# One operand of each later first product made seven steps early into held tiles, and the P2 sum of the second product kept in PSUM over all quarters

## The chip, the core and the metric

The kernel runs on one NeuronCore of a Trainium2 chip. TensorE (PE) multiplies, its weight loads (PEld) overlap the multiplications; ScalarE (ACT) and VectorE (DVE) do the elementwise work, GpSimd (POOL) and SyncE (SP) mostly issue transfers. The metric is the device time of one execution in microseconds (us), the median of the runs. Each engine takes its instructions in the order of its own queue and waits at an instruction whose input is not ready.

## The reference

A model of two layers on 512 tokens of width 1024, in float32. Layer 0 mixes with stick-breaking attention, layer 1 with a gated linear recurrence; after each mixer comes the MLP that this change touches.

```python
def squared_relu_mlp(h, w1, w2):
    u = jax.nn.relu(h @ w1)
    return (u * u) @ w2

def reference(x, norm_mix, norm_mlp, mlp_w1, mlp_w2, ...):
    ...
        x = x + y
        h = rms_norm(x, norm_mlp[layer])
        x = x + squared_relu_mlp(h, mlp_w1[layer], mlp_w2[layer])
    return rms_norm(x, norm_final)
```

`w1` is 1024 x 4096, `w2` is 4096 x 1024, for each layer.

## The kernel before

A float32 product is made of three matmuls of rounded halves. An operand is copied to a rounded high half by ACT (`wh`, `bh`, `sh`: a CAST row), the rest is subtracted by DVE (`wl`, `bl`, `sl`: a TENSOR_TENSOR row), and PE adds high x high, low x high and high x low. `operand` (L1091) does this for a weight block, `split` and `split_slot` for an activation.

The hidden width of 4096 is worked off in four quarters of 1024. In each, the products are done by a scheme with seven block products in place of eight (P1 to P7), which add and subtract blocks: `added` (L1109) adds one block of weights onto another, by DVE (`b<-b,b`) or, for P7 and P4 and one P6, by a POOL transfer that adds. `PRODUCTS` says for each which block of the activations and which blocks of the weights it takes (`b11`, `b12`, `b21`, `b22`), and to which sum it goes: X (P1, P6, P7, P4), V (P5, P3) or W (P2). Only P2 takes `b21`, which no other product needs: `source` (L1100) loads it into a tile of its own, `raw`, of which there are three.

A quarter has 28 steps, counted by `place` (L1186); a layer starts at place 14 of quarter 0, whose first product is done in another way.

- Places 0 to 6 are the first product (up) for the first half of the quarter's hidden width, in the order P1 P5 P6 P3 P7 P2 P4; places 7 to 13 are the same for the second half. A step is 24 matmuls of 256 columns. Each result is read from PSUM by ACT (a COPY row) or by an add on DVE (`u<-ps,u`, `u<-u,ps`), then relu and square on ACT make the activations of the second product, which are split into halves again (`bh`, `bl` for the first half, `sh`, `sl` for the second).
- Places 14 to 27 are the second product (down), with sums over both halves: P1 0, P5 0, P1 1, P2 0, P5 1, P6 0, P6 1, P3 0, P3 1, P7 0, P7 1, P2 1, P4 0, P4 1, where 0 and 1 name the half. A step is 12 matmuls of 512 columns. `collect` (L1140) scales a finished sum and adds it onto the output `c` on DVE (the first time on ACT).

PE's order is written out by `run` (L1172), and the orders of ACT and DVE follow it there too, since each of their instructions in an MLP is issued behind the one before (`Ordered`). For step i, `load(i)` issues transfers, `leave(i - 1)` reads the step before and calls `prepare(i + 3)`, and then PE's matmuls of step i are issued. Leaving step i thus prepares step i + 4: `prepare` (L1220) makes that step's operand (and the one before it, if that was left out: P7's waits for a POOL transfer) and does the additions that the next steps need. A weight operand lives in a ring of four pairs of `wh` and `wl`.

PSUM has eight banks under four names with two each: o, t, a (acc) and z. `bank` (L857) deals them in a fixed turn, `BANKS`. Each quarter takes two for its W sum, and its `collect` at place 25 frees them.

Of the kernel before, what the change touches and what calls it, by code (L numbers as in the profile page):

```python
# [13 lines left out]
F32R = mybir.dt.float32r  # L14
# [4 lines left out]
P = 128  # L19
S = 512  # L20
D = 1024
C = D // P
# [45 lines left out]
def hybrid_encoder(  # L68
# [27 lines left out]
    wpool = ctx.enter_context(tc.tile_pool(name="wpool", bufs=4))  # L96
# [138 lines left out]
    wpools, rawpools = [wpool], [wpool]  # L235
    slabs, loads = count(), count()
# [91 lines left out]
    with ExitStack() as actx:  # L328
# [26 lines left out]
        q, kh, kl, v, w = {}, {}, {}, {}, {}  # L355
# [73 lines left out]
        sums = work.tile([P, S], F32, tag="ssq", name="ssq", bufs=1)  # L429
# [303 lines left out]
        steps = chain(*(g for g, _ in fill))  # L733
# [51 lines left out]
    NQ = DFF // D  # L785
# [22 lines left out]
    class Mlp:  # L808
# [28 lines left out]
        def __init__(self, ctx, layer):  # L837
            self.layer, self.sq, self.first = layer, Squares(), None
            self.V, self.A = Ordered(V), Ordered(A)
            self.mp = ctx.enter_context(tc.tile_pool(name=f"mlp{layer}", bufs=2))  # L840
            self.c = [
                self.mp.tile([P, 2, S], F32, tag=f"c{i}", name=f"c{i}", bufs=1) for i in range(4)
            ]
            self.begun, self.a, self.aside = set(), {}, {}
            self.turns = count(4 * layer)
            self.blocks = ExitStack()
            self.bp = self.blocks.enter_context(tc.tile_pool(name=f"blocks{layer}", bufs=2))
            self.u, self.lows, self.s3, self.slots = {}, {}, {}, None
# [6 lines left out]
            return self.c[t // 2 * 2 + h][:, t % 2, :]  # L855

        def bank(self):  # L857
            tag = self.BANKS[next(self.turns) % 8]
            return bank("acc" if tag == "a" else tag)


# [226 lines left out]
                self.FROM_UP,  # L1088
            )

        def operand(self, raw):  # L1091
            pool = wpools[next(slabs) % len(wpools)]
            wh = pool.tile([P, C, P], F32R, tag="wh", name="wh")
            wl = pool.tile([P, C, P], F32R, tag="wl", name="wl")
            wh, wl = (t.rearrange("p (j k) f -> p j (k f)", j=2) for t in (wh, wl))
            self.A.copy(wh, raw)
            self.V.tensor_tensor(wl, raw, f(wh), ALU.subtract)
            return wh, wl
# [62 lines left out]
        def part(self, sums, name, g, w):  # L1161

            to = self.PRODUCTS[name][3]
            if to not in sums:
                sums[to] = [self.bank() for _ in range(2)]
            for i in range(2):
                self.times(name, g, i, w, sums[to][i], name in ("P1", "P5", "P2"))

        UP = "P1", "P5", "P6", "P3", "P7", "P2", "P4"
        STEPS = 28  # L1170

        def run(self, first, between, end):  # L1172
# [5 lines left out]
            steps = []  # L1178
# [5 lines left out]
            units, ws, sums, us = {("down", 0): first}, {}, {}, {}  # L1184
# [25 lines left out]
            def make(i):  # L1210
                if i >= len(steps):
                    return
                name = steps[i][3]
                ws[i] = made[i] = self.operand(self.source(unit(i), name))

                for before, x in (("P5", "P7"), ("P6", "P4")):
                    if name == before:
                        self.added(unit(i), x)

            def prepare(i):  # L1220

                if i < len(steps) and steps[i][0] == "up" and steps[i][3] == "P7":
                    return
                if i - 1 in range(len(steps)) and i - 1 not in made and i > 2:
                    make(i - 1)
                if i < len(steps) and steps[i][0] == "down":
# [11 lines left out]
            def load(i):  # L1238
                q4, at = steps[i][1], place(i)
                for do in self.aside.get(i, ()):  # L1240
                    do()

                if i == 0:
                    self.turns = count(2)
                elif at == 0:
                    self.turns = count(4)
                    self.u.clear()
                    del self.a[1]
                elif at == 4:
# [12 lines left out]
            def leave(i):  # L1262

                ahead = i + 4
                if i < 0:
                    return
                kind, q4, p, name = steps[i]
                bank = sums[kind, q4, p if kind == "up" else 0][self.PRODUCTS[name][3]]
                if kind == "down":
                    if q4 == 0 and self.s3 and place(i) in self.REPLACE:  # L1270
                        self.replace()
                    apart = p and name == "P2" and self.layer and q4 == NQ - 1
                    if p and not apart:
                        self.collect(name, 0, bank[0])
                    if steps[min(ahead, len(steps) - 1)][0] == "down":
                        add(ahead, 0)
                    if p and not apart:
# [12 lines left out]
                    return  # L1290
# [6 lines left out]
                if keep is not None:  # L1297

                    self.A.copy(cut(u[keep]), three)
                at, x, y, op = {  # L1300
                    "P3": (1, three, cut(u[1]), ALU.subtract),
                    "P7": (2, cut(u[2]), cut(u[3]), ALU.subtract),
                    "P2": (0, cut(u[0]), three, ALU.add),
                    "P4": (3, three, None, None),
                }.get(name, (None,) * 4)
# [36 lines left out]
                elif name in ("P5", "P6") and p:  # L1342
                    n = ("P5", "P6").index(name)
# [20 lines left out]
            for i, (kind, q4, g, name) in enumerate(steps):  # L1364
# [10 lines left out]
                to = self.PRODUCTS[name][3]  # L1375
                new = to not in banks
# [33 lines left out]
    with ExitStack() as mctx:  # L1410
# [7 lines left out]
        def feature(c, tag):  # L1418

            pt = bank(tag)  # L1420
            for t in range(NB):
                PE.transpose(
                    pt[:, t * P : (t + 1) * P], mlp.y(t, c // 4)[:, c % 4 * P : (c % 4 + 1) * P],
                    ident,
                )
            V.tensor_tensor(x[c], x[c], pt, ALU.add)
            last["low"] = halves("mix1", c, x[c])

        def end(ws, xs):
            x_down(0, 0)  # L1430
            for i in range(2):
                for g in range(2):
                    mlp.times("P4", g, i, ws[g], xs[i], False)
                mlp.collect("P4", i, xs[i])
                if i == 0:
                    for c in range(4, C):
                        feature(c, "zzoo"[c - 4])
                        squares.chunk(c, x[c], e=G)

        def between(c):  # L1440
# [35 lines left out]
    with ExitStack() as rctx:  # L1476
# [36 lines left out]
        ps, xc, aa, a0, om, z, gin, pg = ({} for _ in range(8))  # L1513
# [4 lines left out]
        ws = {"c2": third}  # L1518
        raws, fetched, made = {}, count(), count(3)
# [375 lines left out]
```

## Time and profile before

| what | value |
|---|---|
| median of 3 runs (lowest to highest) | 1001.99 us (1001.78 to 1002.32) |
| the profiled execution | 1003.18 us |
| its span, from the first to the last instruction | 1001.3 us |
| an MLP's quarter, place 17 to place 17 | 74.75 us |
| casts of weight blocks `wh<-b` on ACT | 168, 1048 ns each |
| their `wl<-b,wh` on DVE | 168, 1220 ns each |
| loads of `raw` from `w_dn` on SP's queue | 16, 512 KB each, 4.9 us to landing |

A row of the timeline gives the start in us, the duration in us, the engine, the line, the operation, what is written and read, the shape, and in brackets how long the engine was idle before and what it waited for. Much of the MLP has L798, the helper that records every operation, so that its rows are told apart by their tiles. ps_t, ps_acc, ps_o and ps_z are the banks by name. The durations of matmuls overlap; the distance of two starts is what a matmul costs. A row of a window gives the stretch, its length, and for PE, PEld, DVE, ACT and POOL the busy time and the count, then the granted clock and the share of the DMA engines.

### The profile page before, as it was taken

What the parts mean: (1) busy time and instruction counts of PE and PEld (TensorE: products, weight loads), DVE (VectorE), ACT (ScalarE), POOL (GpSimd) and SP (SyncE); (2) the same over time, 40 slices, a digit from 0 to 9 for tenths busy, and PEclk for the clock granted to TensorE, in tenths of its full rate; (3) what the DMA queues carried; (4) which work ended last, traced back from release to release, by engine and by line L of the source; (5) the groups of instructions that cost most, each with busy time, mean ns of one, the idle gap of its engine ahead of it and who ended that gap; (6) DMA issues with size and microseconds to landing.
All of it is one profiled execution on the core that took longest, in us unless ns stands there. A gap on an engine that the chain in (4) does not pass through costs nothing.

```text
span 1001.3 us, 15918 instructions
## 1 busy us (share of the span) xinstructions
PE 983.0 (98%) x5836; PEld 884.0 (88%) x5836; DVE 858.0 (86%) x1152; ACT 715.4 (71%) x1110; POOL 176.4 (18%) x243
## 2 busy tenths in 40 slices
PE   9999999999999999999999999999999999999996
PEld 7889999888878988988988888888889989989985
DVE  6888787848898799799799799986887898998898
ACT  6777676836887774774775699975887774874865
POOL 0454444420000011011011220100011111111111
PEclk9999999999999999999999999999999999999999
DMA  7855454537637767777693474446548877977953
GB/s 230 216 146 148 106 153 109 160 117 256 174 87 198 169 160 198 169 163 194 169 239 88 128 191 126 124 157 223 122 95 219 212 142 202 249 141 199 229 107 106
DMA packets 71902, 165.72 MB, mean 166 GB/s; under 512 B 23824, under 2 KB 25104, under 8 KB 71824
## 3 DMA queue, kind: packets, MB, share of 16 engines
q1 hardware_dynamic: 59424, 123.54, 39.4%
q0 software_dynamic: 11680, 40.38, 24.0%
q8 instruction: 46, 0.75, 0.3%
q10 hardware_dynamic: 720, 0.79, 0.2%
q14 instruction: 32, 0.26, 0.1%
HBM read 139.51 MB, written 6.29 MB: 146 GB/s over the span
## 4 chain that ended last, share of the span: by engine, by line
PE 39%; DVE 25%; ACT 22%; issue 8%; DMA 6%; SPq 0%; ACTq 0%; POOL 0%; DVEq 0%; POOLq 0%
PE ps_t L1135 8%; DVE wl L798 6%; ACT wh L798 6%; PE ps_acc L1135 4%; DVE u L798 4%; ACT u L798 3%; PE ps_acc L1036 3%; DVE b L798 3%; PE ps_acc L257 3%; PE ps_acc L259 3%; PE ps_acc L258 2%; PE ps_z L1135 2%; ACT bh L798 2%; DVE c L798 2%; ACT L798 2%
## 5 line engine op out<-in xcount | busy, mean ns | idle before, releaser
L798 ACT CAST wh<-b 128x1024 fp32r<-128x1024 f32 x168 | 173.7, 1048 | 99.6 <-DVE b L798 50.1
L798 DVE TENSOR_TENSOR wl<-b,wh 128x1024 fp32r<-128x1024 f32 x168 | 203.6, 1220 | 38.9 <-ACT wh L798 38.5
L1113 POOL DMA_DIRECT2D b<-in_w_dn x40 | 35.0, 876 | 339.6 <-DVE b L798 153.1
L1036 PE MATMUL ps_z<-xg,wh 128*128 128x256 f32 x384 | 78.2, 277 | 1.0 <-ACT u L798 1.0
L257 PE MATMUL ps_acc<-xg,wh 128*128 128x512 f32 x200 | 79.1, 395 | 0.0
L259 PE MATMUL ps_acc<-xg,wh 128*128 128x512 f32 x200 | 75.8, 379 | 0.0
L258 PE MATMUL ps_acc<-xg,wl 128*128 128x512 f32 x200 | 75.8, 379 | 0.0
L251 DVE TENSOR_TENSOR wl<-raw,wh 128x512 fp32r<-128x512 f32 (+2 forms) x70 | 62.0, 911 | 15.1 <-ACT wh L249 14.8
L798 ACT ACTIVATE u<-u 128x512 f32<-128x512 f32 x100 | 63.2, 632 | 13.3 <-DVE u L798 11.6
L623 DVE TENSOR_TENSOR_SCAN scan<-keep,later 128x128 f32<-128x128 f32 (+1 forms) x64 | 59.3, 929 | 12.9 <-ACT keep L613 6.5
L1036 PE MATMUL ps_z<-xg,wl 128*128 128x256 f32 x240 | 66.0, 275 | 0.0
L1036 PEld LDWEIGHTS ps_z<-xg,wh 128*128 128x128 f32 x384 | 63.5, 192 | 1.7 <-ACT u L798 1.6
L249 ACT CAST wh<-raw 128x512 fp32r<-128x512 f32 (+2 forms) x70 | 50.5, 757 | 19.1 <-PE ps_acc L259 6.8
L627 POOL TENSOR_TENSOR w<-w,scan 128x128 f32<-128x128 f32 (+1 forms) x64 | 51.6, 807 | 53.6 <-DVE scan L623 50.6
L1036 PE MATMUL ps_acc<-xg,wh 128*128 128x256 f32 x288 | 60.5, 275 | 0.0
L798 DVE TENSOR_TENSOR b<-b,b 128x1024 f32<-128x1024 f32 x48 | 58.7, 1223 | 1.3
L798 DVE TENSOR_TENSOR u<-u 128x512 f32<-128x512 f32 (+1 forms) x92 | 54.8, 595 | 2.3 <-ACT u L798 1.0
L1113 POOL DMA_DIRECT2D b<-in_w_up x24 | 20.9, 869 | 196.8 <-DMA b<-in_w_up 84.4
L1036 PE MATMUL ps_acc<-xg,wl 128*128 128x256 f32 x192 | 52.8, 275 | 0.0
L1036 PE MATMUL ps_acc<-low,wh 128*128 128x256 f32 x192 | 52.8, 275 | 0.0
L798 ACT CAST wh<-raw 128x1024 fp32r<-128x1024 f32 x46 | 47.9, 1043 | 4.1 <-PE ps_acc L1135 4.0
L1135 PE MATMUL ps_t<-wh,sl 128*128 128x512 f32 x126 | 48.5, 385 | 1.9 <-DVE sl L798 1.9
(372 smaller groups left out, 3257.9 us busy)
## 6 DMA issues: line engine op xcount, KB each, us to landing
b<-in_w_dn SPq DMA_DIRECT2D x48, 512.0 KB, 5.1
b<-in_w_dn POOLq DMA_DIRECT2D x40, 512.0 KB, 5.5
b<-in_w_up SPq DMA_DIRECT2D x36, 512.0 KB, 4.7
b<-in_w_up POOLq DMA_DIRECT2D x24, 512.0 KB, 5.8
raw<-in_w_m SPq DMA_DIRECT2D x16, 512.0 KB, 4.7
raw<-in_w_dn SPq DMA_DIRECT2D x16, 512.0 KB, 4.9
raw<-in_w_in SPq DMA_DIRECT2D x16, 512.0 KB, 4.2
raw<-in_w_qk SPq DMA_DIRECT2D x12, 512.0 KB, 3.7
```

The lines of the kernel that those rows point to most:

```text
L249: A.copy(wh[:, k, :], raw[:, k, :])
L251: V.tensor_tensor(wl[:, k, :], raw[:, k, :], f(wh[:, k, :]), ALU.subtract)
L257: PE.matmul(ps, wh, ah, start=start, stop=False)
L258: PE.matmul(ps, wl, ah, start=False, stop=False)
L259: PE.matmul(ps, wh, al, start=False, stop=stop)
L623: V.tensor_tensor_scan(sc[:, S - n : S][:, ::-1], keep[:, :n][:, ::-1], later[:, S - n :][:, ::-1], 1.0, ALU.mult, ALU.max,)
L627: G.tensor_tensor(wt, wt, sc[:, S - n + 1 : S + 1], ALU.mult)
L798: ins = getattr(self.e, name)(*args, **kwargs)
L1036: PE.matmul(as_read(ps[:, i * HS : (i + 1) * HS]), m, turns_of(y), start=new and i == k == n == 0, stop=i == 1 and k == C // 2 - 1 and n == 2,
L1113: G.dma_start(out=unit[b].rearrange("p j n -> p (j n)"), in_=unit["src"](to), accum_op=ALU.add)
L1135: PE.matmul(ps, m, y[:, jj], start=first and n == 0, stop=last and n == 2, skip_group_check=not new,)
```

## The change

Two things are done, in both layers.

**One operand early.** The operand of place 12 (P2 of the second half, quarters 1 to 3) is made when place 5 is left, not place 8. Its halves go to two tiles, `spare`, that are taken once from the three `raw` buffers and held over the quarters. Leaving places 8 to 11 then prepares the step five ahead (so 13, 14, 15 and 16), leaving place 12 prepares nothing, and leaving place 13 goes on as before with 17.

**One sum kept.** The W sum of the second product (P2) stays in its two banks from quarter 0 to 3. The matmuls go on adding, and the `collect` of P2 is left out in quarters 0 to 2. Two banks are so held over the whole MLP (both of z), and the other six are dealt from written lists, `planned`, by quarter. Layer 0's last two transposes before the next mixer (`feature`) take a bank of acc and one of t in place of two of o.

```diff
-            self.turns = count(4 * layer)
+            self.spare = None
+            self.kept, self.growing = None, False
+            self.planned = []
+            self.turns = count(2 + 2 * layer)
...
         def bank(self):
-            tag = self.BANKS[next(self.turns) % 8]
+            tag = self.planned.pop(0) if self.planned else self.BANKS[next(self.turns) % 8]
...
-        def operand(self, raw):
-            pool = wpools[next(slabs) % len(wpools)]
-            wh = pool.tile([P, C, P], F32R, tag="wh", name="wh")
-            wl = pool.tile([P, C, P], F32R, tag="wl", name="wl")
+        def operand(self, raw, spare=False):
+            if spare:
+                self.spare = self.spare or [
+                    wpool.tile([P, C, P], F32R, tag="raw", name="spare", bufs=3) for _ in range(2)
+                ]
+                wh, wl = self.spare
+            else:
+                pool = wpools[next(slabs) % len(wpools)]
+                wh = pool.tile([P, C, P], F32R, tag="wh", name="wh")
+                wl = pool.tile([P, C, P], F32R, tag="wl", name="wl")
...
             if to not in sums:
-                sums[to] = [self.bank() for _ in range(2)]
+                if to == "W":
+                    self.kept = self.kept or [self.bank() for _ in range(2)]
+                sums[to] = self.kept if to == "W" else [self.bank() for _ in range(2)]
+            new = name in ("P1", "P5") or name == "P2" and not self.growing
+            self.growing = self.growing or name == "P2" and g == 1
...
+        SOONER, MADE = 12, 5
...
+                if i in made:
+                    return
...
-                if i - 1 in range(len(steps)) and i - 1 not in made and i > 2:
-                    make(i - 1)
+                for n in range(max(i - 2, 2), min(i, len(steps))):
+                    make(n)
...
                 if i == 0:
-                    self.turns = count(2)
+                    self.planned[:] = "ooatzz"
                 elif at == 0:
-                    self.turns = count(4)
+                    self.planned[:] = ("", "atatooaatoat", "totoaattoa", "oaoattooatat")[q4]
...
-                ahead = i + 4
                 if i < 0:
                     return
+                at = place(i)
+                ahead = i + 4 + (at in range(self.SOONER - 4, self.SOONER))
+                if at == self.MADE:
+                    make(i + self.SOONER - at)
+                if at == self.SOONER:
+                    ahead = len(steps) + 9
...
+                    grows = name == "P2" and q4 < NQ - 1
...
-                    if p and not apart:
+                    if p and not apart and not grows:
                         self.collect(name, 0, bank[0])
```

What this makes of the queues is shown at three places of quarter 2 of layer 0; the other quarters 1 to 3 read alike.

DVE as place 5 is left. `u<-u,ps` is P2's add of the first half, `bl<-u,bh` the first of its halves for the second product, `wl<-b` the splits of P5 and P6 of the second half. Before:

```order
L798 TENSOR_TENSOR wl<-b_4514,wh 128x1024
L798 TENSOR_TENSOR b_4514<-b_4514,b_4570 128x1024
L798 TENSOR_TENSOR u<-u,ps_z 128x2x256
L798 TENSOR_TENSOR wl<-b_4514,wh 128x1024
L798 TENSOR_TENSOR bl<-u,bh 128x2x768
```

and after:

```order
L798 TENSOR_TENSOR wl<-b_4510,wh 128x1024
L798 TENSOR_TENSOR b_4510<-b_4510,b_4566 128x1024
L798 TENSOR_TENSOR spare<-raw,spare 128x1024
L798 TENSOR_TENSOR u<-u,ps_t 128x2x256
L798 TENSOR_TENSOR wl<-b_4510,wh 128x1024
L798 TENSOR_TENSOR bl<-u,bh 128x2x768
```

The split of place 12 now stands ahead of the add.

DVE as places 9 to 12 are left. `u<-ps,u` is P3's add of the second half, the first `u<-u` P7's, `u<-u,ps` P2's; the last row is the `sl` that P1 1 at place 16 takes. Before, from the second `bl` of the first half:

```order
L798 TENSOR_TENSOR bl<-u,bh 128x1024
L798 TENSOR_TENSOR u<-ps_o,u 128x512
L798 TENSOR_TENSOR wl<-b_4750,wh 128x1024
L798 TENSOR_TENSOR b_4750<-b_4750,b_4752 128x1024
L798 TENSOR_TENSOR u<-u 128x512
L798 TENSOR_TENSOR sl<-u,sh 128x2x256
L798 TENSOR_TENSOR wl<-b_4750,wh 128x1024
L798 TENSOR_TENSOR sl<-u,sh 128x2x256
L798 TENSOR_TENSOR u<-u,ps_o 128x512
L798 TENSOR_TENSOR wl<-b_4754,wh 128x1024
L798 TENSOR_TENSOR b_4754<-b_4754,b_4990 128x1024
L798 TENSOR_TENSOR sl<-u,sh 128x2x256
```

and after:

```order
L798 TENSOR_TENSOR wl<-b_4744,wh 128x1024
L798 TENSOR_TENSOR b_4744<-b_4744,b_4746 128x1024
L798 TENSOR_TENSOR bl<-u,bh 128x1024
L798 TENSOR_TENSOR u<-ps_acc,u 128x512
L798 TENSOR_TENSOR wl<-b_4744,wh 128x1024
L798 TENSOR_TENSOR u<-u 128x512
L798 TENSOR_TENSOR sl<-u,sh 128x2x256
L798 TENSOR_TENSOR wl<-b_4748,wh 128x1024
L798 TENSOR_TENSOR b_4748<-b_4748,b_4987 128x1024
L798 TENSOR_TENSOR sl<-u,sh 128x2x256
L798 TENSOR_TENSOR u<-u,ps_acc 128x512
L798 TENSOR_TENSOR sl<-u,sh 128x2x256
```

The split of place 14 and the addition for place 15 (the first two rows) have moved ahead of P3's add, the split of place 16 and the addition for place 18 ahead of P2's, and nothing stands between P2's add and its `sl`.

SP's queue from the loads of place 4 on, where each `raw` load waits for a free buffer. Before:

```order
L1066 DMA b_4754<-in_w_dn 128x1024
L1066 DMA b_4752<-in_w_dn 128x1024
L1105 DMA raw<-in_w_dn 128x1024
L1066 DMA b_4750<-in_w_dn 128x1024
L1066 DMA b_4990<-in_w_dn 128x1024
L1066 DMA b_4992<-in_w_dn 128x1024
L1105 DMA raw<-in_w_up 128x1024
```

and after:

```order
L1069 DMA b_4748<-in_w_dn 128x1024
L1069 DMA b_4746<-in_w_dn 128x1024
L1114 DMA raw<-in_w_up 128x1024
L1069 DMA b_4744<-in_w_dn 128x1024
L1114 DMA raw<-in_w_dn 128x1024
L1069 DMA b_4987<-in_w_dn 128x1024
L1069 DMA b_4989<-in_w_dn 128x1024
```

The load for place 12 has moved into the same quarter, behind two loads of place 4.

More of the change, by code (lines that the diff above doesn't have):

```diff
@@ L1164, in part @@
             if to not in sums:
-                sums[to] = [self.bank() for _ in range(2)]
+                if to == "W":
[3 more added lines that the diff above has]
+            self.growing = self.growing or name == "P2" and g == 1
             for i in range(2):
-                self.times(name, g, i, w, sums[to][i], name in ("P1", "P5", "P2"))
+                self.times(name, g, i, w, sums[to][i], new)
         UP = "P1", "P5", "P6", "P3", "P7", "P2", "P4"
+        SOONER, MADE = 12, 5
         STEPS = 28
@@ L1212, in make @@
                     return
+                if i in made:
+                    return
                 name = steps[i][3]
-                ws[i] = made[i] = self.operand(self.source(unit(i), name))
+                ws[i] = made[i] = self.operand(self.source(unit(i), name), place(i) == self.SOONER)
                 for before, x in (("P5", "P7"), ("P6", "P4")):
@@ L1276, in leave @@
                         add(ahead, 0)
-                    if p and not apart:
+                    if p and not apart and not grows:
                         self.collect(name, 1, bank[1])
@@ L1436, in end @@
                     for c in range(4, C):
-                        feature(c, "zzoo"[c - 4])
+                        feature(c, ("z", "z", "acc", "t")[c - 4])
                         squares.chunk(c, x[c], e=G)
```

## The prediction

> **What bounds the kernel now.** I read the page first, then the windows of one whole quarter of an MLP, then the timeline of TensorE at the end of that quarter's up products, and last the two engines it waits for there.
>
> ```profile
> span 1001.3 us, 15918 instructions
> PE 983.0 (98%) x5836; PEld 884.0 (88%) x5836; DVE 858.0 (86%) x1152; ACT 715.4 (71%) x1110; POOL 176.4 (18%) x243
> 367.93:442.68 74.75, 74.34 (x505) 68.97 (x505) 67.26 (x74) 49.14 (x63) 7.83 (x9) 1.00 0.72 176
> PE ps_t L1135 <- DVE sl L798: 1.9, 6, 0.3
> ```
>
> TensorE is the bound: the third row is one quarter of layer 0, and PE is busy for 74.34 of its 74.75 us at clock 1.00, DVE (67.26) comes next. The change removes no matmul, so it can only alter how long PE waits. The last row, from the list of who waited for whom, says where that happens six times: the down products (ps_t, L1135) wait for an `sl`, once per quarter 1 to 3 of each layer. The timeline of one such place:
>
> ```profile
> 439.01 0.40 PE L1135 MATMUL ps_t<-wh,sh 128*128 128x512 f32 x1
> 439.25 0.38 PE L1135 MATMUL ps_t<-wl,sh 128*128 128x512 f32 x1
> 439.95 0.48 PE L1135 MATMUL ps_t<-wh,sl 128*128 128x512 f32 x1 [0.32 <-DVE sl L798]
> 440.27 0.38 PE L1135 MATMUL ps_t<-wh,sh 128*128 128x512 f32 x1
> ...
> 442.21 0.38 PE L1135 MATMUL ps_z<-wh,bh 128*128 128x512 f32 x1
> 442.68 0.48 PE L1135 MATMUL ps_z<-wl,bh 128*128 128x512 f32 x1
> 443.00 0.38 PE L1135 MATMUL ps_z<-wh,bl 128*128 128x512 f32 x1
> ```
>
> The first row is where place 16 begins (P1, second half), the 442.21 row where place 17 begins (P2). Matmuls overlap, so a wait is read from starts: undisturbed, one starts 0.216 us after another (the 12 of place 16 take 442.21 - 439.01 = 3.20 us; without the waits that follow, 2.6 = 12 x 0.216). From 439.25 to 439.95 are 0.70, so 0.48 of wait for `sl`, and 0.10 more at the next start (0.32); from 442.21 to 442.68 are 0.47, so 0.25 of wait for `wl`, and again 0.10. **0.94 us a quarter**, 5.6 us in six: this is all that the change can win at this place. It comes from DVE and ACT, which hand work to each other there:
>
> ```profile
> 413.19 1.23 DVE L798 TENSOR_TENSOR b<-b,b 128x1024 f32<-128x1024 f32 x1
> 414.34 0.68 DVE L798 TENSOR_TENSOR u<-u,ps_z 128x512 f32<-128x512 f32 x1
> ...
> 418.30 1.76 DVE L798 TENSOR_TENSOR bl<-u,bh 128x1536 fp32r<-128x1536 f32 x1 [1.47 <-ACT bh L798]
> ...
> 425.02 1.22 DVE L798 TENSOR_TENSOR wl<-raw,wh 128x1024 fp32r<-128x1024 f32 x1
> 426.16 1.22 DVE L798 TENSOR_TENSOR bl<-u,bh 128x1024 fp32r<-128x1024 f32 x1
> ...
> 429.56 0.69 DVE L798 TENSOR_TENSOR u<-ps_o,u 128x512 f32<-128x512 f32 x1
> 430.17 1.22 DVE L798 TENSOR_TENSOR wl<-b,wh 128x1024 fp32r<-128x1024 f32 x1
> 431.42 1.23 DVE L798 TENSOR_TENSOR b<-b,b 128x1024 f32<-128x1024 f32 x1
> 432.56 0.68 DVE L798 TENSOR_TENSOR u<-u 128x512 f32<-128x512 f32 x1
> ...
> 435.60 0.69 DVE L798 TENSOR_TENSOR sl<-u,sh 128x512 fp32r<-128x512 f32 x1 [0.61 <-ACT sh L798]
> 436.21 0.68 DVE L798 TENSOR_TENSOR u<-u,ps_o 128x512 f32<-128x512 f32 x1
> ...
> 439.21 0.69 DVE L798 TENSOR_TENSOR sl<-u,sh 128x512 fp32r<-128x512 f32 x1
> 440.06 1.42 DVE L798 TENSOR_TENSOR u<-u 128x512 f32<-128x512 f32 x2 [0.17 <-ACT u L798]
> 441.40 1.22 DVE L798 TENSOR_TENSOR wl<-raw,wh 128x1024 fp32r<-128x1024 f32 x1
> ```
>
> ```profile
> 414.51 1.06 ACT L798 CAST wh<-b 128x1024 fp32r<-128x1024 f32 x1 [1.42 <-DVE b L798]
> 415.47 1.28 ACT L798 ACTIVATE u<-u 128x512 f32<-128x512 f32 x2
> ...
> 430.29 1.30 ACT L798 ACTIVATE u<-u 128x512 f32<-128x512 f32 x2 [1.03 <-DVE u L798]
> 431.61 0.62 ACT L798 CAST sh<-u 128x512 fp32r<-128x512 f32 x1
> ...
> 436.93 1.30 ACT L798 ACTIVATE u<-u 128x512 f32<-128x512 f32 x2 [0.40 <-DVE u L798]
> 438.26 0.62 ACT L798 CAST sh<-u 128x512 fp32r<-128x512 f32 x1
> 438.78 0.59 ACT L798 ACTIVATE u<-ps_z 128x512 f32<-128x512 f32 x1
> 439.40 0.63 ACT L798 ACTIVATE u<-u 128x512 f32<-128x512 f32 x1
> ```
>
> From 418.30 to 435 DVE has no pause to speak of, yet it takes up the second half's P2 sum (`u<-u,ps_o`) only at 436.21, five us after PE finished it (place 12 ended at 439.01 - 2 x 2.6 - 2.69 = 431.1, an up place being 24 matmuls of 0.112). Behind that add hangs a chain: relu and square, the cast `sh`, then `sl`. PE wants `sh` at 439.01. **The time at which P2's add starts decides the wait.**
>
> **The change, part by part.** I follow DVE through the new order of its queue (the rows under "The change") with the durations above.
>
> *The early split.* Leaving place 5, the operand of place 12 is now cast by ACT and split by DVE ahead of P2's add of the first half. ACT has room: 1.42 us idle before 414.51, the cast takes 1.05. On DVE it stands in front of the add of 414.34 and holds the queue for 1.14 (from 425.02 to 426.16), so the add starts at 415.48 and ends at 416.16. ACT's relu, which ran at 415.47, starts at 416.19: 0.72 later, and with it the cast `bh` and the `bl` of 418.30, now 419.02. The idle 1.47 before that `bl` does not cover it, since that idle time is the wait for this same chain.
>
> *From there to P3's add.* It was 429.56 - 418.30 = 11.26 us of queue. Gone is the place-12 split (1.14). New is the split of place 14 and the addition for place 15, because leaving places 8 to 11 prepares five ahead, not four: 432.56 - 430.17 = 2.39. P3's add starts at 419.02 + 11.26 - 1.14 + 2.39 = 431.53, 1.97 later than before.
>
> *From P3's add to P2's.* It was 436.21 - 429.56 = 6.65, of which 0.61 idle, so 6.04 of work. The new order has the same kinds (two splits, one addition, two `sl`, two adds): 6.04 again. Idle comes in twice. The first `sl` needs `sh`, which is 1.94 behind the end of P3's add (430.29 to 431.61 + 0.62) with 0.04 for each hand-over: 431.53 + 0.69 + 0.04 + 1.94 + 0.04 = 434.24, DVE would be free at 433.87, so 0.37. The next split needs ACT's cast behind that `sh`: another 0.35. P2's add starts at 431.53 + 6.04 + 0.72 = **438.29, where it was 436.21**.
>
> *The wait.* From that add's start to the end of `sh` were 438.26 + 0.62 - 436.21 = 2.67, a chain that no reordering shortens: `sh` is there at 440.96. PE, at place 16 since 439.01, waits 1.95 for it. `sl` ends 0.73 after it, PE wants it 0.43 after: 0.30 more, and 0.10 as above. ACT's relu and square of P4 start 0.52 behind the start of `sh` and end at 442.11; the two sums take 1.34 (440.06 to 441.40), the split of place 17 ends at 443.49 + 1.22 = 444.71. PE begins place 17 at 440.96 + 0.40 + 2.59 = 443.95 and wants that `wl` 0.22 later: 0.58 with its hand-over, and 0.10. Together 3.03 where 0.94 were: **2.09 us a quarter**. The next quarter starts from PE again (DVE has pauses before it, below), so nothing adds up from one to the next: 6 x 2.09 = 12.5 us.
>
> *The kept sum.* Twelve collects go (two in each of quarters 0 to 2 of both layers), a pair taking 394.20 - 392.88 = 1.32 us of DVE.
>
> ```profile
> 392.88 1.40 DVE L798 SCALAR_TENSOR_TENSOR c<-ps_z,rr,c 128x512 f32<-128x512 f32 x2
> 394.20 1.22 DVE L798 TENSOR_TENSOR wl<-b,wh 128x1024 fp32r<-128x1024 f32 x1
> ...
> 397.86 1.23 DVE L798 TENSOR_TENSOR wl<-b,wh 128x1024 fp32r<-128x1024 f32 x1 [1.19 <-ACT wh L798]
> ...
> 403.44 1.23 DVE L798 TENSOR_TENSOR wl<-b,wh 128x1024 fp32r<-128x1024 f32 x1 [1.90 <-ACT wh L798]
> ```
>
> Between them and the up products DVE already pauses for 1.19 and 1.90 us, and PE does not wait: the time falls into a pause. At most it is worth 6 x 1.32 = 7.9 us, if DVE bound there; I take nothing, by the two pauses. Against it stand two banks fewer in turn. The tightest reuse is place 15's second bank, read last by P3's add (ends 432.2 in the new order) and written by PE from 439.01 - 1.3 = 437.7: 5.5 us to spare, nothing again, where a late release would cost PE what it is late.
>
> *One load buffer.* The held tiles take two of the three `raw` slots, so from quarter 2 on the place-12 operand is loaded only when that of place 5 is split.
>
> ```profile
> 401.57 3.45 SPq L1066 DMA_DIRECT2D b<-in_w_dn  x2
> 405.83 0.33 SPq L1105 DMA_DIRECT2D raw<-in_w_dn  x1
> DMA to landing us min/median/max: 4.3/4.4/5.2
> ```
>
> A load is issued at that very point before too, at 405.83, and those of this stretch land within 5.2: 411.0, and ACT wants it at 413.1. It costs nothing with 2 us to spare; behind the waiting cast would stand the relu of 415.47, and each us of lateness beyond would reach PE whole.
>
> *A rule against it.* The windows row grants clock 1.00, and after each wait above the matmuls go on at 0.22 (439.01 to 439.25). The Trainium skill, "TensorE: Matmul & The Clock Gate" (Part 1: The HAM clock gate), says that TensorE falls to half its clock once it was idle for a window of about 3.4 us. By that rule the forecast waits of about 2 us leave the clock alone; by none of the rows here can it be tried, as no wait is as long.
>
> **The rivals.** (1) *The waits go* and nothing replaces them: 6 x 0.94 less, 996.4 us. For it: place 12 has no split left to prepare, and `sl` now stands right behind P2's add. It decides by one point: P2's add must start by 439.01 - 2.67 = 436.34. My chain misses that by two us, and DVE would have to find them between 418 and 436, where it has none. (2) *Nothing measurable*: P2's add lands within some 0.3 us of its old place, because the removed split and the pulled ones cancel: 1002.0. Against it: 2.39 came in, 1.14 went. (3) *Half of it*: the early split slips into a pause and the 0.72 is not passed on; then 1.37 a quarter, 8.2, 1010.2. Against it: the order rows put it ahead of the add, and ACT's cast cannot start before 413.1. (4) *The change does not get its operand early*: the one buffer makes the load late by 1 us or so in the four later quarters, 1018.5. For it: the two loads of 401.57 to 405.0 are still under way when it starts. (5) *The clock*: if a wait of more than three us halves TensorE's rate over the next place of 2.59 us, 6 x 2.59 come on top, 1030.
>
> **How the numbers follow.** The profiled execution took 1003.18 us with its span of 1001.30; 12.5 more are 1015.7. The median of the runs shown is 1001.99, 1.19 below the profiled one, so 1014.5. Chances: forecast (1011 to 1018) 0.68, (3) 0.11, (1) 0.09, (4) 0.06, (2) 0.04, (5) 0.02. Slower by over 0.2% (about what a measurement of this kernel can tell from no change) is forecast, (3), (4) and (5): 0.87; within it 0.04; faster 0.09. The range 1008 to 1019 holds the forecast, most of (3) and part of (4).
>
> **What would show it.** In the profile after: PE's first matmul of place 16 waits for ACT `sh` (not `sl`) about 1.9 us, six times; P2's add of the second half starts within half a us of its `sl` chain with DVE idle some 2 us between them; `c<-ps_z` appears only in the last quarters; place 5 shows a split ahead of `u<-u,ps`. It would be wrong if DVE reached P3's add before 430 in the frame above, if the wait for `sh` is absent, or if PE waits for a bank or a load instead.

## The result, and the profile after

The change makes the kernel slower. Its median is 1018.88 us (1017.25 to 1021.22, four runs); before it was 1002.15 (1001.78 to 1002.64, four runs beside them). The ratio is 1.0168, 95% interval 1.0148 to 1.0189. The profiled execution is the fastest of the four, 1017.25 us.

The head of its page, and the window of one quarter of layer 0 from its place 0 to the next (the columns as before):

```profile
span 1014.7 us, 15901 instructions
PE 985.8 (97%) x5836; PEld 885.3 (87%) x5836; DVE 851.9 (84%) x1140; ACT 715.2 (70%) x1110; POOL 176.4 (17%) x243
395.50:472.20 76.70, 75.22 (x505) 69.18 (x504) 66.08 (x72) 49.25 (x62) 7.85 (x9) 1.00 0.69 172
```

DVE has twelve instructions fewer and is 6 us less busy, PE has the same 5836 matmuls at the same clock, and each quarter is about 2 us longer. The time went into waits of PE. The list of who waited for whom has rows that before had only small ones like them:

```profile
PE ps_o L1039 <- ACT u L798: 4.5, 4, 2.2
PE ps_acc L1039 <- ACT u L798: 2.9, 4, 1.3
PE ps_z L1144 <- DVE wl L798: 2.7, 7, 0.4
PE ps_t L1039 <- ACT u L798: 2.6, 6, 1.2
...
PE ps_acc L1144 <- ACT sh L798: 1.3, 2, 0.6
PE ps_o L1144 <- ACT sh L798: 1.0, 2, 0.6
PE ps_t L1144 <- ACT sh L798: 1.0, 2, 0.6
```

The rows with `sh` are the forecast wait at place 16. Those at L1039 are not in the forecast: they stand in the up products and wait for ACT's `u`. Such a row gives only the idle part of a wait, so all waits are counted here from the distances of starts (0.216 us for 512 columns, 0.112 for 256, undisturbed), from place 0 to place 18 of each quarter 1 to 3. In us, worked out from all starts of PE in the two traces:

| quarter | before | after | more | after, by place |
|---|---|---|---|---|
| layer 0, 1 | 1.67 | 3.57 | 1.90 | 9: 0.77, 11: 0.48, 13: 0.50, 16: 1.18, 17: 0.64 |
| layer 0, 2 | 0.93 | 2.92 | 1.99 | 9: 0.13, 11: 0.48, 13: 0.49, 16: 1.18, 17: 0.64 |
| layer 0, 3 | 0.96 | 2.93 | 1.97 | 9: 0.14, 11: 0.48, 13: 0.49, 16: 1.18, 17: 0.64 |
| layer 1, 1 | 2.41 | 4.30 | 1.89 | 9: 1.48, 11: 0.49, 13: 0.49, 16: 1.19, 17: 0.65 |
| layer 1, 2 | 1.14 | 6.15 | 5.01 | 9: 2.42, 11: 2.17, 16: 0.91, 17: 0.65 |
| layer 1, 3 | 1.20 | 4.52 | 3.32 | 9: 1.53, 11: 1.43, 16: 0.91, 17: 0.65 |
| sum | 8.31 | 24.39 | 16.08 | |

The 16.08 us account for the 16.73 between the medians. (The profiled spans differ by 13.4 only: the first piece of the program, which both kernels share, ran 2.0 us shorter in the profiled execution after, and the second product of layer 0's quarter 0 ran 0.8 us shorter.) Four quarters lose 1.9 to 2.0 each; two quarters of layer 1 lose more.

DVE after, in the same stretch as in the prediction. Quarter 2 of layer 0 runs 0.82 us earlier in this trace (before's `b<-b,b` of 413.19 is the first row), so 0.82 is added where times are compared:

```profile
412.37 1.23 DVE L798 TENSOR_TENSOR b<-b,b 128x1024 f32<-128x1024 f32 x1
413.51 1.22 DVE L798 TENSOR_TENSOR spare<-raw,spare 128x1024 fp32r<-128x1024 f32 x1
414.65 0.68 DVE L798 TENSOR_TENSOR u<-u,ps_t 128x512 f32<-128x512 f32 x1
...
418.21 1.76 DVE L798 TENSOR_TENSOR bl<-u,bh 128x1536 fp32r<-128x1536 f32 x1 [1.74 <-ACT bh L798]
...
427.21 1.22 DVE L798 TENSOR_TENSOR wl<-b,wh 128x1024 fp32r<-128x1024 f32 x1
428.46 1.23 DVE L798 TENSOR_TENSOR b<-b,b 128x1024 f32<-128x1024 f32 x1
...
430.74 0.69 DVE L798 TENSOR_TENSOR u<-ps_acc,u 128x512 f32<-128x512 f32 x1
...
437.40 0.68 DVE L798 TENSOR_TENSOR u<-u,ps_acc 128x512 f32<-128x512 f32 x1
440.09 0.69 DVE L798 TENSOR_TENSOR sl<-u,sh 128x512 fp32r<-128x512 f32 x1 [2.01 <-ACT sh L798]
```

The early split stands ahead of P2's add of the first half, the pulled split and addition (427.21, 428.46) ahead of P3's add, and P2's add of the second half starts at 437.40, or 438.22 in the frame of before, where it was 436.21. ACT and PE in the same quarter:

```profile
424.87 0.58 ACT L798 COPY u<-ps_o 128x512 f32<-128x512 f32 x1
...
429.77 1.05 ACT L798 CAST wh<-b 128x1024 fp32r<-128x1024 f32 x1 [2.43 <-DVE b L798]
430.73 0.58 ACT L798 COPY u<-ps_o 128x512 f32<-128x512 f32 x1
...
439.44 0.62 ACT L798 CAST sh<-u 128x512 fp32r<-128x512 f32 x1
```

```profile
425.01 0.28 PE L1039 MATMUL ps_acc<-low,wh 128*128 128x256 f32 x1
425.50 0.38 PE L1039 MATMUL ps_o<-xg,wh 128*128 128x256 f32 x1 [0.22 <-ACT u L798]
...
431.36 0.38 PE L1039 MATMUL ps_o<-xg,wh 128*128 128x256 f32 x1 [0.23 <-ACT u L798]
...
440.11 0.48 PE L1144 MATMUL ps_t<-wh,sh 128*128 128x512 f32 x1 [0.63 <-ACT sh L798]
```

Before, ACT's copies after P6 and after P7 in this quarter:

```profile
424.96 0.58 ACT L798 COPY u<-ps_z 128x512 f32<-128x512 f32 x1
...
428.67 0.59 ACT L798 COPY u<-ps_z 128x512 f32<-128x512 f32 x1 [0.28 <-PE ps_z L1036]
```

Places 9, 11 and 13 (P6, P7, P4) go on adding in the bank that the X sum stands in, here ps_o. ACT must have copied the state after P1, P6 and P7 out of it first, and these copies stand in ACT's queue. The copy of 430.73 stands behind a weight cast that the five-ahead order put there, and that cast waits 2.43 us for DVE's addition (428.46); PE starts place 13 0.05 us after the copy's end. The copy of 424.87 is at 425.69 in the frame of before, where it was at 424.96: the 0.73 by which the early split put off P2's add and all behind it. So PE loses 0.48 at place 11 and 0.49 at 13, though a row shows 0.22 and 0.23 of idle time, and arrives at place 16 about 1.1 us late already. There it waits that much less for `sh`. It is not the two banks fewer: with eight banks in their old turn (the early operand alone, below) places 9, 11 and 13 wait the same 1.1 us in this quarter.

### The profile page after: what moved, and what is told of

Same layout as the page of the kernel before. It is cut to its first block, busy times and chain, and to the rows that moved or that the text cites. A ratio compares the mean times of both kernels' runs of the same rounds, so it can differ in the third digit from the quotient of the medians.

```text
span 1014.7 us, 15901 instructions
## 1 busy us (share of the span) xinstructions
PE 985.8 (97%) x5836; PEld 885.3 (87%) x5836; DVE 851.9 (84%) x1140; ACT 715.2 (70%) x1110; POOL 176.4 (17%) x243
## 4 chain that ended last, share of the span: by engine, by line
PE 31%; DVE 27%; ACT 19%; issue 15%; DMA 6%; POOL 1%; SPq 1%; ACTq 0%; DVEq 0%; POOLq 0%
DVE wl L798 8%; ACT wh L798 4%; PE ps_o L1144 3%; DVE b L798 3%; DVE c L798 3%; ACT u L798 3%; DVE u L798 3%; DMA b<-in_w_up 3%; PE ps_acc L257 3%; PE ps_acc L259 3%; PE ps_acc L258 3%; PE ps_acc L1144 2%; DVE sl L798 2%; DVE bl L798 2%; ACT L798 2%
## 5 line engine op out<-in xcount | busy, mean ns | idle before, releaser
L1039 PE MATMUL ps_o<-xg,wh 128*128 128x256 f32 x224 | 46.2, 277 | 4.5 <-ACT u L798 4.5
L798 DVE TENSOR_TENSOR sl<-u,sh 128x512 fp32r<-128x512 f32 (+2 forms) x50 | 37.5, 751 | 14.1 <-ACT sh L798 14.1
L1039 PE MATMUL ps_acc<-xg,wh 128*128 128x256 f32 x224 | 46.2, 277 | 2.9 <-ACT u L798 2.9
L1039 PE MATMUL ps_t<-xg,wh 128*128 128x256 f32 x224 | 46.3, 278 | 2.6 <-ACT u L798 2.6
L798 DVE TENSOR_TENSOR bl<-u,bh 128x1024 fp32r<-128x1024 f32 (+2 forms) x26 | 33.9, 1303 | 12.8 <-ACT bh L798 12.8
L798 ACT CAST wh<-raw 128x1024 fp32r<-128x1024 f32 x40 | 41.5, 1040 | 4.1 <-PE ps_acc L1144 1.6
L617 POOL TENSOR_SCALAR_AFFINE_SELECT w<-w 128x128 f32<-128x128 f32 x64 | 32.5, 507 | 65.4 <-ACT w L612 65.1
L259 PEld LDWEIGHTS ps_acc<-xg,wh 128*128 128x128 f32 x200 | 37.8, 189 | 5.4
```

Source lines behind the costliest of these rows:

```text
L259: PE.matmul(ps, wh, al, start=False, stop=stop)
L617: G.affine_select(t, t, pattern=[[-1, P]], compare_op=ALU.is_gt, fill=0.0, base=0, channel_multiplier=1,)
L798: ins = getattr(self.e, name)(*args, **kwargs)
L1039: PE.matmul(as_read(ps[:, i * HS : (i + 1) * HS]), m, turns_of(y), start=new and i == k == n == 0, stop=i == 1 and k == C // 2 - 1 and n == 2,
```

## The experiments

Three theories were tried. **A**: the order of DVE's queue makes P2's chain late (the prediction's); **B**: the one load buffer that is left makes the load of place 12's operand late; **C**: six banks in place of eight make PE wait. What PE loses in each kernel is put into one table behind the last run.

**The kept sum alone** (no early split, no pulled steps, three `raw` buffers).

```diff
-        SOONER, MADE = 12, 5
+        SOONER, MADE = -99, -99
```

> The kept P2 sum and the written bank lists alone; place 12 is prepared four steps ahead as before, with three raw buffers. Theory A (the cost is the order of DVE's queue: operands pulled one step ahead and the early split): no change, 1002 us within 0.2%, and PE waits 0.94 us at places 16 and 17 of a quarter as before. Theory B (one raw buffer makes loads late): also 1002. Theory C (six banks in turn, so PE waits for a bank): 1010 or more, with waits of PE for ACT copies at places 9 to 13. If the twelve collects had stood on the path: 994 to 1000.

Measured 1003.2 us (11 runs; before beside it 1002.55, 15 runs), ratio 1.0008 (1.0000 to 1.0017). PE's waits in the six quarters are 7.85 us, before 8.31. Neither the 7.9 us that the collects took on DVE nor a wait for a bank shows: in the old order the kept sum with its bank lists is worth nothing, and C falls.

**The early operand alone** (every quarter collects, the banks in their old turn).

```diff
...
-            new = name in ("P1", "P5") or name == "P2" and not self.growing
+            new = name in ("P1", "P5", "P2")
...
-                    grows = name == "P2" and q4 < NQ - 1
+                    grows = False
...
```

> The early operand with its held tiles and the five-ahead preparation alone; P2's sum is collected in every quarter and the banks are dealt in the old turn. Theory A and B: as the whole change, 1016 to 1020 us, P2's add of the second half some 7 us after PE ended place 12, PE waits about 2.9 us a quarter in layer 0. Theory C: near 1002.

1020.22 us, 0.2 above the expected 1016 to 1020, ratio 1.0183 (1.0168 to 1.0199): the whole loss is in this part. PE loses 26.35 us; the 2 us more than in the change are in layer 1, about 0.7 in quarter 2 and 1.2 in quarter 3. In quarter 2 one wait for a copy is followed by a lowered clock, by which PE loses 1.6 us (the first matmul behind the wait; the next run has such a wait too, with its clock):

```profile
876.52 0.58 PE L1039 MATMUL ps_z<-xg,wh 128*128 128x256 f32 x1 [2.88 <-ACT u L798]
```

**Four ahead, the split still at place 5.** Only the pulling of the steps behind goes.

```diff
-                ahead = i + 4 + (at in range(self.SOONER - 4, self.SOONER))
+                ahead = i + 4
...
-                if at == self.SOONER:
-                    ahead = len(steps) + 9
```

> The whole change, but every step is prepared four ahead again (places 8 to 12 as before, with place 12's operand already there). The early split still stands ahead of P2's add of the first half at place 5. Theory A: what was pulled ahead (2.39 us of DVE ahead of P3's add) is the cost, and it is gone; the early split delays by 0.72 and the missing split of place 12 gives back 1.14, so PE waits about 0.8 to 1.0 us a quarter in layer 0, as before, and the time is 1002 plus what late loads cost in layer 1 (2 to 5 us): 1003 to 1007. Theory B (the loads are the whole cost): 1014 or more. Theory C: 1014 or more.

1007.51 us, ratio 1.0058 (1.0045 to 1.0070), 0.5 us above the expected 1003 to 1007. In layer 0, quarters 2 and 3, PE's waits fall from 2.93 to 0.90 (before, 0.93 and 0.96); but they stand elsewhere, 0.14 at place 9, 0.47 at place 11 and 0.29 at place 17, none at place 16. So the five-ahead order costs the 2 us a quarter, by A. The early split by itself removes the wait for `sl` and gives the same time back at the copies. What is left of the loss is in layer 1, quarter 2 above all: 3.84 of its 4.24 us at place 9. ACT stood 2.67 us at the cast of the early operand, for its load, and the copy for place 9 stands behind that cast. That is B. But not all of it is wait; ACT's row, PE's rows there, and the windows behind them (clock third from the end):

```profile
862.38 1.06 ACT L798 CAST spare<-raw 128x1024 fp32r<-128x1024 f32 x1 [2.67 <-DMA raw<-in_w_up]
...
869.62 0.38 PE L1039 MATMUL ps_o<-xg,wh 128*128 128x256 f32 x1 [2.38 <-ACT u L798]
...
870.84 0.30 PE L1039 MATMUL ps_o<-xg,wl 128*128 128x256 f32 x1
...
871.15 0.42 PE L1039 MATMUL ps_o<-xg,wh 128*128 128x256 f32 x1
871.36 0.42 PE L1039 MATMUL ps_o<-xg,wl 128*128 128x256 f32 x1
```

```profile
868.00:870.00 2.00, 0.38 (x3) 0.39 (x4) 1.83 (x2) 2.00 (x4) 0.00 (x0) 1.00 0.84 134
870.00:872.00 2.00, 2.00 (x15) 2.00 (x15) 1.97 (x3) 1.97 (x4) 0.00 (x0) 0.74 1.07 274
872.00:874.00 2.00, 2.00 (x11) 2.00 (x11) 1.93 (x4) 0.27 (x2) 0.00 (x0) 0.50 1.10 226
874.00:876.00 2.00, 2.00 (x18) 2.00 (x18) 2.00 (x2) 2.00 (x3) 0.00 (x0) 0.91 0.62 222
```

After 2.38 us without work PE goes on at full rate, and from 870.95 to 874.35 at half: 16 starts take 3.40 us where they would take 1.79. **1.6 of the 4.2 us are a lowered clock**, not a wait.

**The split at place 8, where it was before, five ahead kept.**

```diff
-        SOONER, MADE = 12, 5
+        SOONER, MADE = 12, 8
```

> The whole change with the operand of place 12 made when place 8 is left, not place 5, so in its old place in the queues; the five-ahead preparation stays. Theory A: the cost is the five-ahead preparation, so layer 0 stays slow, about 3.0 to 3.3 us of PE's wait a quarter; the load has 8 us more, so that layer 1's quarters 2 and 3 cost the same as layer 0's: 1014 to 1017 us. Theory B: near 1002, since no load is late any more. Theory C: as the whole change.

1017.1 us, ratio 1.0148 (1.0135 to 1.0162). The four plain quarters wait 0.4 us longer than after (3.34 and 3.37 in layer 0's last two), and quarters 2 and 3 of layer 1 now wait like them (3.59 and 3.54 in place of 6.15 and 4.52). The time is just above the expected 1014 to 1017. Without the early split the pulled steps still carry 14.6 of the 16.7 us, and the load is in time when it is wanted three places later. The 0.4 us are what the prediction's terms give: with the split back in its old place neither its 0.72 nor the 1.14 that it freed stands in the sum.

**Without the residual's fetches 4 and 7.** In layer 1, `fetch` brings a part of the residual from memory in many small pieces, on SP's queue too. This kernel leaves out the fetches 4 and 7, which run in quarters 2 and 3, so that two of the eight blocks added to the output hold something else.

```diff
+            if n in (4, 7):
+                return
```

> The whole change without eight of the 32 small fetches of the residual in layer 1: those of blocks 4 and 7, which run at places 2 to 5 of quarters 2 and 3, so that two of the eight blocks that are added to the output hold something else. If the late load of place 12's operand comes from these fetches on the same queue and the same transfer engines, it lands in time: layer 1's quarters 2 and 3 then make PE wait 2.9 us each, as layer 0's do, not 6.2 and 4.5, and the time falls by some 3 to 5 us, to 1014 to 1016. If it is the one raw buffer or the order of the queue by itself that makes the load late, the waits stay near 6.2 and 4.5 us and the time near 1018.

1016.28 us, ratio 1.0133 (1.0119 to 1.0147), between the two expectations. With the fetches, the change has these rows in layer 1, quarter 2: SP's queue, the transfer of `raw` (KB and us to landing) and ACT.

```profile
856.20 2.04 SPq L1069 DMA_DIRECT2D b<-in_w_dn  x1
858.34 1.14 SPq L1114 DMA_DIRECT2D raw<-in_w_up  x1
859.57 3.40 SPq L1721 DMA_DIRECT2D bl<-away  x3
```

```profile
raw<-in_w_up SPq DMA_DIRECT2D x1, 512.0 KB, 8.7
```

```profile
867.03 1.06 ACT L798 CAST spare<-raw 128x1024 fp32r<-128x1024 f32 x1 [2.43 <-DMA raw<-in_w_up]
...
879.26 1.05 ACT L798 CAST wh<-b 128x1024 fp32r<-128x1024 f32 x1 [2.48 <-DMA b<-in_w_up]
```

The load is issued among the fetches (L1721), takes 8.7 us to landing, and ACT's cast waits 2.43 us for it. Without the two fetches ACT casts `spare` without a pause, and quarters 2 and 3 wait 4.03 and 3.53 us. So late transfers, by the traffic of these fetches, are shown to cost 2.12 and 0.99 us of these two quarters. That is B, but not B alone, since the transfer of the second cast above came sooner too: in quarter 2 PE's wait falls from 2.42 to 0.7 us at place 9, behind the cast of `spare`, and from 2.17 to 1.8 at place 11, behind the second cast. It is not all of their excess either, as that second transfer stays late in quarter 2, here ACT's row without the fetches:

```profile
880.23 1.05 ACT L798 CAST wh<-b 128x1024 fp32r<-128x1024 f32 x1 [2.07 <-DMA b<-in_w_up]
```

This is POOL's adding transfer for place 13, which five ahead wants a place sooner. No run took that transfer away.

**The split in the quarter before.** If the place in DVE's queue decides, the split should go where DVE pauses and not ahead of the copies. It is made when place 25 of the quarter before is left, four ahead otherwise, the sum kept.

```diff
-        SOONER, MADE = 12, 5
+        SOONER, MADE = 12, 25
...
-                ahead = i + 4 + (at in range(self.SOONER - 4, self.SOONER))
-                if at == self.MADE:
-                    make(i + self.SOONER - at)
-                if at == self.SOONER:
-                    ahead = len(steps) + 9
+                ahead = i + 4
+                if at == self.MADE and i + self.SOONER + 28 - at < len(steps):
+                    make(i + self.SOONER + 28 - at)
```

> The whole change with two differences: every step is prepared four ahead, and the operand of place 12 is made when place 25 of the quarter before is left, where DVE pauses, not at place 5. Theory A (DVE's queue between place 5 and place 16 sets the wait): 1.14 us leave that stretch and nothing comes in, P2's add of the second half starts at about 435.4 in the frame of the kernel before (it was 436.2), PE's waits at places 11 to 17 fall from 0.94 to 0.1 us in layer 0, and the time is 996 to 999 us if the load of place 5's operand, now issued after this split, lands in time. If the held tiles themselves cost something: 1002 or more.

997.75 us (995.87 to 999.92), ratio 0.9951 (0.9938 to 0.9964), **faster than both kernels**. Its window of the quarter and DVE at the end of the quarter before:

```profile
392.90:466.80 73.90, 73.90 (x505) 69.09 (x504) 66.12 (x72) 49.16 (x62) 7.86 (x9) 1.00 0.72 178
```

```profile
389.43 1.22 DVE L798 TENSOR_TENSOR spare<-raw,spare 128x1024 fp32r<-128x1024 f32 x1
...
394.37 1.23 DVE L798 TENSOR_TENSOR wl<-b,wh 128x1024 fp32r<-128x1024 f32 x1 [1.19 <-ACT wh L798]
...
399.99 1.22 DVE L798 TENSOR_TENSOR wl<-b,wh 128x1024 fp32r<-128x1024 f32 x1 [1.94 <-ACT wh L798]
```

PE is busy in all of the 73.90 us. The split (389.43) takes the time that a pair of collects took, the two pauses of 1.19 and 1.94 us are still there, and nothing behind them is late. P2's add of the second half starts at 435.42 in the frame of before, where 435.4 was expected and 436.21 was measured before. Only 0.17 of wait is left in this quarter, at place 17.

**The same at place 26.**

```diff
-        SOONER, MADE = 12, 25
+        SOONER, MADE = 12, 26
```

> As the one before, with the operand made when place 26 is left, 2.6 us later. Theory A: the same 0.1 us at places 11 to 17, but the load of place 5's operand has 2.6 us less, so that in layer 1 it may be late by 0 to 2 us in quarters 2 and 3, seen as a wait of PE at places 3 to 9: 996 to 1002 us.

999.47 us, ratio 0.9967 (0.9954 to 0.9979). The intervals of the two overlap; a step later does not help.

**The split at place 25 with the collects back.**

```diff
...
-                    grows = name == "P2" and q4 < NQ - 1
+                    grows = False
...
```

(and the banks in their old turn, as in the second run).

> As the one made at place 25, without the kept sum: P2 of the second product is collected in every quarter and the banks go in the old turn. Theory A: DVE has pauses after place 25 that take both the collects and the split, so within 0.2% of the one with the kept sum. If it is over 2 us slower, the kept sum is worth that much once the split has moved there.

1004.38 us, ratio 1.0018 (1.0009 to 1.0027): the expectation missed. The kept sum (with its bank lists), worth nothing alone, is worth 6.6 us here. DVE and ACT of this kernel; its quarter begins at 396.9, 4.0 us later than in the rows of the split at place 25 with the sum kept (392.9):

```profile
393.49 1.22 DVE L798 TENSOR_TENSOR spare<-raw,spare 128x1024 fp32r<-128x1024 f32 x1
394.63 1.40 DVE L798 SCALAR_TENSOR_TENSOR c<-ps_z,rr,c 128x512 f32<-128x512 f32 x2
...
404.05 1.23 DVE L798 TENSOR_TENSOR wl<-b,wh 128x1024 fp32r<-128x1024 f32 x1 [0.76 <-ACT wh L798]
...
407.90 1.23 DVE L798 TENSOR_TENSOR wl<-b,wh 128x1024 fp32r<-128x1024 f32 x1 [1.49 <-ACT wh L798]
```

```profile
406.82 2.08 ACT L798 CAST wh<-b 128x1024 fp32r<-128x1024 f32 x2 [1.07 <-DMA b<-in_w_up]
```

The pair of collects (394.63) now stands behind the early split. The pause that was 1.94 us is 0.76 (404.05): the 1.3 us of collects and the 1.2 of the split do not both fit. What comes behind is late by a transfer too, POOL's addition into `b`, for which ACT waits 1.07; then DVE waits 1.49, and the copies for places 9 and 11 cost PE 0.58. This chain is read from one trace; no run took the transfer away by itself, and none gave back the collects with the bank lists left as they were.

All kernels: what PE loses in the six quarters, by the distances of its starts in one trace each, against the time (us more than before, from the medians of each batch):

| kernel | lost | more lost | more time |
|---|---|---|---|
| before | 8.31 | | |
| the change | 24.39 | 16.1 | 16.7 |
| kept sum alone | 7.85 | -0.5 | 0.7 |
| early operand alone | 26.35 | 18.0 | 17.7 |
| four ahead | 11.70 | 3.4 | 5.0 |
| split at place 8 | 22.51 | 14.2 | 14.6 |
| no fetches 4 and 7 | 21.04 | 12.7 | 13.7 |
| split at 25 of the quarter before | 3.20 | -5.1 | -4.8 |
| the same at 26 | 3.60 | -4.7 | -3.1 |
| at 25, collects back | 9.03 | 0.7 | 1.8 |

The losses in these stretches carry the result of each kernel to within 2 us.

## Why the prediction was right, and where it was not

*The early split, the pulled steps, P2's add.* Right, row by row. In the frame of before: P2's add of the first half at 415.47 (forecast 415.48), `bl` at 419.03 (419.02), P3's add at 431.56 (431.53), P2's add at 438.22 (438.29), the end of `sh` at 440.88 (440.96). DVE idles 2.01 us before its `sl`, as forecast. That the pulled steps carry the loss was then shown by two runs: without them the waits of layer 0 fall to 0.90 us, and with them and no early split they are 3.3 and 3.4.

*The wait.* Its sum was right, its place was not. The forecast put 3.03 us a quarter at places 16 and 17; it is 2.92 in layer 0, quarter 2, but only 1.18 and 0.64 of it there. The step that failed is "PE, at place 16 since 439.01": it took PE's up products as undisturbed and followed ACT only for `u<-u`, `bh` and `sh`. ACT's copies out of the X bank stand in the same queue, behind the same late work, and PE needs each before it may go on in that bank. They cost 1.10 us at places 9, 11 and 13, which the wait for `sh` gives back, since the end of `sh` is set by DVE and ACT and not by PE. That the sum still came out is by this give and take, which the prediction did not see. Its first sign to look for, about 1.9 us of wait for `sh` six times, was thus not seen (0.5 to 0.6 us idle in each row; all of place 16 loses 1.2, or 0.9 in layer 1's last two quarters). PE waiting for a bank, which it named as a sign of being wrong, was seen in part: a wait for a copy is a wait for the bank.

*The sum over six quarters.* Four quarters lose 1.94 us on average where 2.09 were forecast: 7.8 of the 8.4 us.

*One load buffer.* This is the term that was mis-sized. It was taken at nothing for all quarters, by a landing of 5.2 us at most and 2 us to spare, from rows of layer 0. That holds for layer 0, where the load of quarter 2 takes 5.4 us to landing and ACT has it in time. In quarters 2 and 3 of layer 1 the load goes out among the residual's fetches, takes 8.7 us in quarter 2, and the quarters lose 5.01 and 3.32 where the others lose 1.94: 4.5 us beyond. Taking the fetches away gave 3.1 of them back, in part through POOL's transfers; the rest is in part POOL's transfer for place 13, shown as a wait but not taken away. It is the mechanism of rival (4), about two us in each of two quarters where that rival had one in each of four. These 4.5 us are as much as the whole distance from the forecast's 1014.5 to 1018.88. The time lies above the forecast's own 1011 to 1018, just inside the wider 1008 to 1019, and 0.4 us from the 1018.5 of rival (4), which was given 0.06; the forecast's own sum missed by this one term.

*The kept sum.* Taken at nothing, and alone it is worth nothing. But the reason given, that its 1.32 us fall into a pause, holds only while nothing else fills the pause: with the split at place 25 the same collects, with the bank turn that goes with them, cost 6.6 us. In the change as it stands, the early operand alone against both gives 1.0183 against 1.0168, with overlapping intervals.

*The other rivals.* (1), the waits go: its point of decision was P2's add at 436.34, which it missed by 1.9 us. The run that puts the split a quarter ahead makes them go, at 997.75 where the rival had 996.4. (2) falls with the same add, which is 2.0 us later than before and not within 0.3, and (3) with the rows behind the early split, which was passed on in full. (5), the clock, did not come in the change: its longest wait is 2.16 us of idle time, in layer 1's quarter 2, and the matmuls behind it keep their rate. (The prediction's starts for that rate, 439.01 and 439.25, are 0.24 apart and stand ahead of the wait; behind it, 440.27 and 440.48 are 0.21 apart and show the same.)

```profile
874.26 0.38 PE L1039 MATMUL ps_o<-xg,wh 128*128 128x256 f32 x1 [2.16 <-ACT u L798]
874.47 0.28 PE L1039 MATMUL ps_o<-xg,wl 128*128 128x256 f32 x1
```

But its mechanism is there in two of the experiments. Of all starts of 256- and 512-column matmuls in the ten traces, those behind two waits are at half rate for about 3.4 us: 2.38 us idle in the run with four ahead, 2.88 in the early operand alone. Each cost 1.6 us, less than the 2.59 of the rival.

## What to carry to other kernels

Making one operand earlier does not free an in-order engine: ask what it is put ahead of, and what else is moved up to fill its old place, because here the pulled successors cost most of the time: with them back in their places 5.0 of the 16.7 us are left, most of it in layer 1 by the late load. A pause can be filled once, so an edit that is worth nothing alone can be what pays for another, and two such edits should be tried together in the place where the engine pauses. And follow every reader that a queue holds, the copies that merely release an accumulator too, in each stage with its own traffic, not in one stage for all.

## What was unexpected of the hardware

The clock fell after shorter waits than was thought: not after 2.16 us of idle time, but after 2.38, and there 1.3 us behind the wait; after 2.88 at once: the starts behind the row of 876.52 are 0.21 us apart where 0.11 is usual, and the granted clock from 878 to 880 us is 0.52. Both times it was back some 3.4 us later. The 3.4 us bear out the length that the Trainium skill, "TensorE: Matmul & The Clock Gate" (Part 1: The HAM clock gate) gives for its window; but it speaks of a whole idle window, and here a wait of 0.7 of one was enough (2.38 of 3.4 us, of which 2.1 lie in the 3.4 us that end at the fall, at 870.95). Which share of a window decides was not tried.

A 512 KB load that took 5.4 us to landing in layer 0 took 8.7 us when it was issued among 64 KB fetches and POOL's transfers, and issuing held SP's queue longer as well: 1.14 us for this load and 2.04 for the one ahead of it, against 0.33 each in layer 0. Without the fetches 4 and 7 the load was issued in 0.33 us and landed after 6.1. This load in both views in layer 0, quarter 2:

```profile
405.03 0.33 SPq L1114 DMA_DIRECT2D raw<-in_w_up  x1
```

```profile
raw<-in_w_up SPq DMA_DIRECT2D x1, 512.0 KB, 5.4
```

The idle time that a PE row shows is less than what the wait costs: 0.22 us where the distance of the starts, 0.49 in place of 0.11, and the longer first matmul behind it took 0.48 together. Waits counted by idle time alone would have found about half of this result at places 11 and 13.
